# Products of a pair added in PSUM, two of them issued among the next pair's, in a hybrid decoder block

## The chip, the cores and the metric

The kernel runs on one core of a Trainium2 chip. The metric is the device time of one execution in microseconds (us), the median of several runs. Everything is float32 at the boundary; the matrix products are made of float32r parts, as told below.

## What is computed

One decoder layer on 1024 positions of width 1024:

```python
u  = rmsnorm(x)
P  = u @ W_in            # [gate_a | gate_s | B_a | C_a | v_a | z | xBC | dt]
A  = W_a_out( B_a * causal_dwconv3( C_a * v_a ) )
S  = W_s_out( GroupRMSNorm( SSD(conv4(xBC)) * silu(z) ) )
h  = x + W_o( sigmoid(gate_a) * A + sigmoid(gate_s) * S )
v  = rmsnorm(h)
h  = h + W_down( silu(causal_dwconv3(v W_1) + b) * (v W_3) )
out = rmsnorm(h)
```

SSD is the chunked state-space scan: 32 heads in 4 groups, 8 chunks of 128 positions. The inner width of z and of the x part of xBC is 2048, that of the feed-forward part 2816.

## The kernel before

**Tiling.** Channels lie on the 128 partitions, positions along the free axis, so a projection makes one tile of 128 channels by 1024 positions. Two such tiles, a *pair*, are made together. The pair is a 2 by 2 block product (two halves of the contraction, two halves of the positions, two output tiles) done with seven block products instead of eight, in the manner of Strassen and Winograd. The combinations of the activations (a11, a12, a22, s1 to s4; `COMBOS`, L195) are made once for u and once for v. The combinations of the weights (t1 to t4, by L295, L296, L297 and L314 on POOL) are made for each pair.

**A product** (`product`, L253) is twelve matmuls of 128x128 by 128x512. Each operand is split in a high float32r part (a cast on ACT, L148) and the rest (a subtraction on POOL or DVE, L149), and hi x hi, hi x lo and lo x hi are added over four slices of the contraction. The split weights go to one of 13 buffers ("w"), so about six products can be prepared ahead.

**A pair** (`Pair`, L265) loads its first raw weight tile r1 when it is made. `first` runs a11 and a12: a11 is copied out of PSUM by ACT (L285, m1), and DVE adds a12 to it (L287). `operands` loads r2 and makes t1 to t3. `second` runs s1, s2, s3, a22 and s4, and DVE adds the seven results up as it takes them out of PSUM (L308, L311, L312, L313, L316, L318). Each product has a PSUM bank of its own. There are 8 banks: four tagged "mm" (a11, a12, s2, s3) and four tagged "sd" (s1, a22, s4, and all that the SSD chunks need: px, pb, pc, pd, po, pst, pn, pr).

**Which pairs there are.** Three gate pairs at the head (`head`, whose first two products run while u is still being prepared), 8 pairs in `BEFORE`, 29 in `BESIDE`, then, after the output projections, 22 feed-forward pairs (names "up"; `ffn_first`, L969, and the loop at L1010). The kinds in the mixer: xb (xBC, followed by a convolution of four taps on DVE, L539, and silu, and written to memory `ssd_in`), z (silu, also to `ssd_in`), ca (names "cv": C_a and v_a, product and three taps), ba (times ca's result, to `tad`), gs and ga (gates, tanh; tile names "g" and gt). Output tiles live in pools: "s4", 3 buffers (xb, ca's product, ba, also the sums of W_down and the first tile of a feed-forward pair), and "b4", 3 buffers in the mixer (z, gates, convolved tiles). "c2" has 6 half tiles, "t2" 3, raw weights ("raw") 3 buffers of a whole tile.

**SSD beside the pairs.** `BESIDE` is the stretch in which SSD chunks run between products. A clock (`tick`, L328) counts products. Chunk s has its stages at ticks `D0 + DSTEP * s` plus an offset from `STAGES` (L54): loads of the decay matrix m (from `acd`, issued on ACT's queue) and of its inputs (from `ssd_in`) 9 ticks ahead, the relu and exp of m on ACT (L642, L643) 6 ahead, transposes (px, L648) 4 ahead, the matmuls pd, po and pst (L690 to L703) at 0, the sums of squares 3 behind and the norm (pn, L733; a power on POOL, L739; pr, L743) 6 behind. The chunk's number c needs the tiles of its group: for group 0 those are xb 0 to 3, 16 and 20 and z 0 to 3.

**After the mixer.** `y_a` (L816) and `s_out` (L852) are the output projections of A and S, `out_proj` (L882) that of the merge. Beside them runs `w_sums` (L789): it loads two tiles of W_down into two "s4" tiles, combines them on DVE and POOL (L784, L787; tile name wd) and writes them to `td`. After the feed-forward pairs come four sweeps (names d) for W_down.

**What sets the order.** Each engine runs its own queue strictly in order. A planner makes the queues when the program is built: it goes by the order of the program text as a priority and by when operands, buffers and banks would be ready in its own estimate of times. An instruction that comes early in an engine's queue but waits for something late holds all that stands behind it. Loads of weights and stores are issued on SP's queue, the SSD's loads and the stores of convolved tiles and gates on ACT's.

## Time and profile before

| | |
|---|---|
| median of 3 runs | 2004.32 us (2004.31 to 2005.55) |
| the profiled execution | 2004.03 us |
| its span, first to last instruction | 2002.3 us |
| mean granted clock of TensorE | 0.986 |
| head and mixer pairs on PE | to 987 us |
| y_a, s_out, out_proj on PE | 988 to 1347 us |
| feed-forward pairs on PE | 1351 to 1782 us |
| W_down on PE | 1782 to 1994 us |

The page of a profile gives each engine's busy time (PE is TensorE's matmuls, PEld its weight loads, DVE VectorE, ACT ScalarE, POOL GpSimd, SP the engine that only issues here). A row of a window gives, for a stretch of time, the busy time and number of instructions of PE, PEld, DVE, ACT and POOL, the clock granted to TensorE (1.00 is full), the mean busy share of the DMA engines and what they moved. A row of waits reads: engine, tile and line that waited, what ended the wait, the sum of those waits in us, how many, the longest. A row of the timeline gives start, duration, engine, line, operation, tiles (out<-in), shapes, count, and in brackets the idle time of the engine just before it and what ended it. Tile names carry the pair's kind: pt2xb is the product s2 of an xb pair, pb11cv the product a11 of a ca pair, pt4 is a22, pb22 is s4, pt1 is s1.

### The profile page before, as it was taken

The numbers are of one execution on the slowest core, as the hardware profiler recorded it, in microseconds if no ns is written. First come the engines' busy times: TensorE is split into PE (matmuls) and PEld (weight loads), VectorE is DVE, ScalarE is ACT, GpSimd is POOL, SyncE is SP. The second block draws the span as 40 slices with busy tenths as digits, with TensorE's granted clock in tenths as the row PEclk, the third lists the DMA queues.
The fourth block names the chain that finished last, engine by engine and source line by source line (L and its number), as shares of the span: only waits on it lengthen the run. The fifth ranks groups of instructions, "written<-read, shape, count | busy, mean of one in ns | idle before, by whom it ended". The sixth has DMA issues, their size and how long they took to land.

```text
span 2002.3 us, 26005 instructions
## 1 busy us (share of the span) xinstructions
PE 1923.3 (96%) x8986; PEld 1575.2 (79%) x8986; DVE 1450.9 (72%) x1616; ACT 918.0 (46%) x1697; POOL 1292.9 (65%) x931
## 2 busy tenths in 40 slices
PE   6899989999999999998999999988999999999998
PEld 5778877788788778776788888877888888887886
DVE  8956886787888778786884724379877788884445
ACT  5354445556655855444443323354433333343434
POOL 7667776776767677677545423368887888853542
PEclk9999999999999999999999999998999999999999
DMA  4244234444534554387897645442322244477654
GB/s 153 51 141 143 95 121 153 148 152 144 190 119 151 167 168 144 113 267 254 317 409 251 225 151 188 159 165 81 130 85 102 104 153 153 153 242 261 217 184 157
DMA packets 180179, 338.46 MB, mean 169 GB/s; under 512 B 15280, under 2 KB 87760, under 8 KB 179024
## 3 DMA queue, kind: packets, MB, share of 16 engines
q1 hardware_dynamic: 93264, 253.95, 37.1%
q10 hardware_dynamic: 86784, 82.85, 13.0%
q8 instruction: 71, 1.16, 0.2%
q14 instruction: 60, 0.49, 0.1%
HBM read 247.34 MB, written 89.41 MB: 168 GB/s over the span
## 4 chain that ended last, share of the span: by engine, by line
PE 64%; DVE 14%; DMA 7%; issue 5%; POOL 4%; ACT 4%; ACTq 0%; SPq 0%; POOLq 0%; DVEq 0%
PE so L259 9%; PE ya L259 4%; DVE cv L539 4%; PE pt2up L259 3%; PE pt3up L259 3%; PE pb22up L259 3%; PE pt4up L259 3%; PE pb11up L259 3%; PE pt1up L259 3%; PE pb21up L259 3%; PE d L1031 2%; PE d L1032 2%; PE d L1033 2%; DMA wd<-in_w_down 1%; PE wo L904 1%
## 5 line engine op out<-in xcount | busy, mean ns | idle before, releaser
L539 DVE SCALAR_TENSOR_TENSOR cv<-xbc,scw,cv 128x1024 f32<-128x1024 f32 x72 | 128.8, 1800 | 20.8 <-ACT cv L535 20.5
L642 ACT ACTIVATE m<-m,tk 128x128 f32<-128x128 f32 x256 | 79.1, 391 | 101.0 <-DMA m<-acd 88.5
L539 DVE SCALAR_TENSOR_TENSOR fcv<-fci,fcw,fcv 128x1024 f32<-128x1024 f32 x44 | 85.9, 1953 | 28.5 <-ACT fcv L535 28.5
L149 POOL TENSOR_TENSOR l_ws<-raw_ws,h_ws 128x512 fp32r<-128x512 f32 x32 | 46.4, 1450 | 74.6 <-PE so L259 43.1
L148 ACT CAST h_ws<-raw_ws 128x512 fp32r<-128x512 f32 x64 | 39.4, 622 | 99.1 <-PE so L259 67.5
L259 PE MATMUL so<-yh,h_ws 128*128 128x512 f32 x256 | 68.8, 391 | 0.0
L259 PE MATMUL so<-yl,h_ws 128*128 128x512 f32 x256 | 68.6, 389 | 0.0
L259 PE MATMUL so<-yh,l_ws 128*128 128x512 f32 x256 | 68.5, 389 | 0.0
L149 POOL TENSOR_TENSOR l_wo<-raw_wo,h_wo 128x512 fp32r<-128x512 f32 x24 | 31.6, 1316 | 53.9 <-PE wo L905 36.5
L149 DVE TENSOR_TENSOR l_wo<-raw_wo,h_wo 128x512 fp32r<-128x512 f32 x24 | 25.2, 1050 | 51.7 <-ACT h_wo L148 26.9
L661 ACT ACTIVATE xe<-px,tk 128x64 f32<-128x64 f32 x256 | 55.5, 326 | 13.2 <-DVE xd L654 13.2
L148 ACT CAST h_wo<-raw_wo 128x512 fp32r<-128x512 f32 x48 | 29.6, 621 | 65.5 <-PE wo L905 32.7
L149 DVE TENSOR_TENSOR l_ws<-raw_ws,h_ws 128x512 fp32r<-128x512 f32 x32 | 26.0, 816 | 41.6 <-PE so L259 27.7
L259 PEld LDWEIGHTS so<-yl,h_ws 128*128 128x128 f32 x256 | 48.1, 188 | 10.0
L259 PEld LDWEIGHTS so<-yh,l_ws 128*128 128x128 f32 x256 | 48.1, 188 | 10.0
L259 PEld LDWEIGHTS so<-yh,h_ws 128*128 128x128 f32 x256 | 47.8, 188 | 9.7
L672 DVE TENSOR_TENSOR m<-m,cb 128x1024 f32<-128x1024 f32 x32 | 52.6, 1644 | 0.4
L149 POOL TENSOR_TENSOR l_wa<-raw_wa,h_wa 128x512 fp32r<-128x512 f32 x16 | 27.3, 1704 | 37.7 <-ACT h_wa L148 18.5
L903 PE MATMUL wo<-h_wo,mh 128*128 128x512 f32 x128 | 49.9, 391 | 1.2 <-ACT h_wo L148 1.2
L546 ACT ACTIVATE cv<-cv 128x1024 f32<-128x1024 f32 x24 | 25.5, 1062 | 55.1 <-DVE cv L539 55.1
L904 PE MATMUL wo<-l_wo,mh 128*128 128x512 f32 x128 | 50.0, 391 | 0.0
L905 PE MATMUL wo<-h_wo,ml 128*128 128x512 f32 x128 | 49.7, 391 | 0.0
(1063 smaller groups left out, 6710.4 us busy)
## 6 DMA issues: line engine op xcount, KB each, us to landing
m<-acd ACTq DMA_DIRECT2D x32, 512.0 KB, 5.5
raw_ws<-in_w_s_out SPq DMA_DIRECT2D x32, 512.0 KB, 4.2
ssd_in<-cv ACTq DMA_DIRECT2D x24, 512.0 KB, 2.6
in<-ssd_in ACTq DMA_DIRECT2D x32, 384.0 KB, 4.1
raw_wo<-in_w_o SPq DMA_DIRECT2D x24, 512.0 KB, 3.4
wd<-in_w_down SPq DMA_DIRECT2D x22, 512.0 KB, 6.1
td<-wd SPq DMA_DIRECT2D x44, 256.0 KB, 4.3
raw_1up<-in_w_up SPq DMA_DIRECT2D x22, 512.0 KB, 3.2
```

The source lines that it names most:

```text
L148: act.copy(hi, v)
L149: (eng or pool).tensor_tensor(lo, v, f32(hi), op=ALU.subtract)
L259: pe.matmul(ps, wt[:, k, :], ct[:, k, :], start=(start and n == 0), stop=(stop and n == 11),)
L539: dve.scalar_tensor_tensor(cv, ci[:, j : j + SEQ], w[:, j : j + 1], cv, op0=ALU.mult, op1=ALU.add)
L642: act.activation(m[:, h, :], m[:, h, :], AF.Relu, bias=a)
L661: act.activation(xe[:, hc], px[:, hc], AF.Copy, scale=tk[:, 2, cc, q, g * HG + h : g * HG + h + 1],)
L672: dve.tensor_tensor(m, m, cb.unsqueeze(1).to_broadcast([P, HG, P]), op=ALU.mult)
L903: pe.matmul(pss[t], mh, wh, start=k == 0, stop=False)
L904: pe.matmul(pss[t], mh, wl, start=False, stop=False)
L905: pe.matmul(pss[t], ml, wh, start=False, stop=k == NK - 1)
L1031: pe.matmul(ps, aa[0][:, ts], bb[0], start=k == 0, stop=False)
L1032: pe.matmul(ps, aa[0][:, ts], bb[1], start=False, stop=False)
```

## The change

- A pair's products are added in PSUM. a11, s2, s3 and a22 go into one "mm" bank one after the other (t4 has its sign turned, so that a22 is added too); ACT copies the running sum out after a11, s2, s3 and a22 (`so_far`). s1 and s4 share another "mm" bank. a12 has an "sd" bank. What DVE still adds is a12 (to the copy of a11), s1 to the sum after s3, and the bank of s1 and s4 to the sum after s2. The copy of a11 goes into the output tile itself (`hold`). Pairs whose first products run early (three at the head, two feed-forward) don't hold the bank of a11: it is copied to m1 as before, s2 opens a new bank, and DVE adds m1 to each running sum.
- The order of products is a11, a12, the previous pair's a22, s2, the previous pair's s4, s1, s3 (`then`); a pair's last two products, and what is done with its outputs (`done`), come in the next pair. `then(None)` closes the mixer's and the feed-forward part's row of pairs.
- t1, t3 and t4 are made in place, over the raw weights, t4 with the others; "t2" has one buffer, "raw" four. `y_a` takes its gh from "c2".
- `BEFORE` has 6 pairs and `BESIDE` 31, in another order, three of the five gate pairs between the other kinds instead of all at the end; `D0` is 17 instead of 11.

```diff
--- before
+++ after
@@ -31,7 +31,7 @@
 GA, GS, BA, CA, VA, ZZ, XB, BB, CB = 0, 8, 16, 24, 32, 40, 56, 72, 76
 NIN = 80 * P
-NRAW, NW, NBIG, NB4, NC2, NT2, NROW = 3, 13, 14, 3, 6, 3, 6
+NRAW, NW, NBIG, NB4, NC2, NT2, NROW = 4, 13, 14, 3, 6, 1, 6
 LO_DVE = ("t1", "b22")
...
@@ -40,17 +40,17 @@
 BEFORE = (
-    ("xb", 16), ("z", 0), ("xb", 18), ("z", 2), ("xb", 20), ("xb", 22), ("xb", 0), ("xb", 2),
+    ("xb", 16), ("z", 0), ("xb", 20), ("xb", 0), ("z", 2), ("xb", 2),
 )
 BESIDE = (
-    ("xb", 4), ("z", 4), ("xb", 6), ("z", 6), ("ca", 0), ("ca", 1), ("ba", 0),
-    ("xb", 8), ("z", 8), ("xb", 10), ("z", 10), ("ca", 2), ("ca", 3), ("ba", 2),
-    ("xb", 12), ("z", 12), ("xb", 14), ("z", 14), ("ca", 4), ("ca", 5), ("ba", 4),
-    ("ca", 6), ("ca", 7), ("ba", 6), ("gs", 0), ("gs", 2), ("gs", 4), ("gs", 6), ("ga", 6),
+    ("xb", 4), ("z", 4), ("xb", 6), ("z", 6), ("xb", 18), ("gs", 0), ("xb", 22), ("z", 8),
+    ("xb", 8), ("z", 10), ("xb", 10), ("gs", 2), ("ca", 0), ("ca", 1), ("ba", 0), ("z", 12),
+    ("xb", 12), ("z", 14), ("xb", 14), ("gs", 4), ("ca", 2), ("ca", 3), ("ba", 2),
+    ("ca", 4), ("ca", 5), ("ba", 4), ("ca", 6), ("ca", 7), ("ba", 6), ("gs", 6), ("ga", 6),
 )
-D0, DSTEP = 11, 6
+D0, DSTEP = 17, 6
 STAGES = LOAD_M, LOAD_IN, DECAY, TRANS, LOAD_Z, DIAG, SQUARES, NORM = -9, -9, -6, -4, -3, 0, 3, 6
...
@@ -250,7 +250,8 @@
             dve.tensor_tensor(a12[i], a12[i], s1[i], op=ALU.subtract)
             put("s4", i, a12[i])
-    def product(ps, c, w, start=True, stop=True):
+    def product(ps, c, w, start=True, stop=True, held=False):
         hi, lo = (t.rearrange("p (k c) -> p k c", k=4) for t in w)
         n = 0
...
@@ -258,69 +259,108 @@
             for k in range(4):
                 pe.matmul(
                     ps, wt[:, k, :], ct[:, k, :],
-                    start=(start and n == 0), stop=(stop and n == 11),
+                    start=(start and n == 0), stop=(stop and n == 11), skip_group_check=held,
                 )
                 n += 1
     class Pair:
-        def __init__(self, A, src1, src2, name, pool=None):
+        def __init__(self, A, src1, src2, name, d1, d2=None, done=None, pool=None):
             self.A, self.src2, self.name = A, src2, name
+            self.d1, self.d2, self.done = d1, d2, done
             self.r1 = load(src1, f"1{name}", pool)
-        def prod(self, c, v, nm, f=mm_tile):
+            self.started = False
+        def prod(self, c, v, nm, ps=None):
             name = self.name
-            ps = f(f"p{nm}{name}")
+            new = ps is None
+            if new:
+                ps = (sd_tile if nm == "b21" else mm_tile)(f"p{nm}{name}")
             eng = dve if nm in LO_DVE else pool
-            product(ps, self.A[c], wsplit(v, f"{nm}{name}", eng))
+            product(ps, self.A[c], wsplit(v, f"{nm}{name}", eng), new, held=True)
             tick()
             return ps
-        def first(self, d1, late=False):
-            self.d1 = d1
+        def first(self, late=False, hold=True):
+            self.started = True
             p = self.prod("a11", self.r1[:, :HALF], "b11")
-            self.m1 = c2(f"m1{self.name}")
+            self.m1 = self.d1[:, :HALF] if hold else c2(f"m1{self.name}")
             act.copy(self.m1, p)
+            self.hold, self.u = hold, p if hold else None
             p = self.prod("a12", self.r1[:, HALF:], "b21")
-            dve.tensor_tensor(d1[:, :HALF], self.m1, p, op=ALU.add)
+            dve.tensor_tensor(self.d1[:, :HALF], self.m1, p, op=ALU.add)
             if not late:
                 self.operands()
         def operands(self):
-            name, b11 = self.name, self.r1[:, :HALF]
-            self.r2 = load(self.src2, f"2{name}")
-            self.t1, self.t2, self.t3 = (t2(f"t{i}{name}") for i in (1, 2, 3))
-            pool.tensor_tensor(self.t1, self.r2[:, :HALF], b11, op=ALU.subtract)
-            pool.tensor_tensor(self.t2, self.r2[:, HALF:], self.t1, op=ALU.subtract)
-            pool.tensor_tensor(
-                self.t3, self.r2[:, HALF:], self.r2[:, :HALF], op=ALU.subtract
-            )
-        def second(self, d2):
-            name, m1, d1 = self.name, self.m1, self.d1
-            b21, t1, tb = self.r1[:, HALF:], self.t1, self.t2
-            b22 = self.r2[:, HALF:]
-            p5 = self.prod("s1", t1, "t1", sd_tile)
-            p = self.prod("s2", tb, "t2")
-            u2 = c2(f"u2{name}")
-            dve.tensor_tensor(u2, m1, p, op=ALU.add)
-            p = self.prod("s3", self.t3, "t3")
-            u3 = c2(f"u3{name}")
-            dve.tensor_tensor(u3, u2, p, op=ALU.add)
-            dve.tensor_tensor(u2, u2, p5, op=ALU.add)
-            dve.tensor_tensor(d2[:, HALF:], u3, p5, op=ALU.add)
-            pool.tensor_tensor(tb, tb, b21, op=ALU.subtract)
-            p = self.prod("a22", tb, "t4", sd_tile)
-            dve.tensor_tensor(d1[:, HALF:], u3, p, op=ALU.subtract)
-            p = self.prod("s4", b22, "b22", sd_tile)
-            dve.tensor_tensor(d2[:, :HALF], u2, p, op=ALU.add)
-    def pair(A, src1, src2, name, d1, d2):
-        p = Pair(A, src1, src2, name)
-        p.first(d1)
-        p.second(d2)
+            name = self.name
+            r1, r2 = self.r1, load(self.src2, f"2{name}")
+            (b11, b21), (b12, b22) = ([r[:, h] for h in halves] for r in (r1, r2))
+            self.t1, self.t2, self.t3, self.t4, self.b22 = b11, t2(f"t2{name}"), b12, b21, b22
+            pool.tensor_tensor(self.t1, b12, b11, op=ALU.subtract)
+            pool.tensor_tensor(self.t2, b22, self.t1, op=ALU.subtract)
+            pool.tensor_tensor(self.t3, b22, b12, op=ALU.subtract)
+            pool.tensor_tensor(self.t4, b21, self.t2, op=ALU.subtract)
+        def so_far(self, o):
+            if self.hold:
+                act.copy(o, self.u)
+            else:
+                dve.tensor_tensor(o, self.m1, self.u, op=ALU.add)
+        def s2(self):
+            self.u = self.prod("s2", self.t2, "t2", self.u)
+            self.u2 = c2(f"u2{self.name}")
+            self.so_far(self.u2)
+        def s1(self):
+            self.v = self.prod("s1", self.t1, "t1")
+        def s3(self):
+            self.prod("s3", self.t3, "t3", self.u)
+            u3 = c2(f"u3{self.name}")
+            self.so_far(u3)
+            dve.tensor_tensor(self.d2[:, HALF:], u3, self.v, op=ALU.add)
+        def a22(self):
+            self.prod("a22", self.t4, "t4", self.u)
+            self.so_far(self.d1[:, HALF:])
+        def s4(self):
+            self.prod("s4", self.b22, "b22", self.v)
+            dve.tensor_tensor(self.d2[:, :HALF], self.u2, self.v, op=ALU.add)
+            self.done()
+    last = [None]
+    def then(p):
+        q, last[0] = last[0], p
+        if p is None:
+            q.a22()
+            q.s4()
+        elif p.started:
+            p.s2()
+            if q is not None:
+                q.a22()
+            p.s1()
+            if q is not None:
+                q.s4()
+            p.s3()
+        else:
+            p.first()
+            q.a22()
+            p.s2()
+            q.s4()
+            p.s1()
+            p.s3()
     slots, clock = {}, [None]
...
@@ -433,11 +473,11 @@
         for t in (4 + j, 5 + j):
             u_norm(t)
         fill_second(U, [(xs[t], t - 4) for t in (4 + j, 5 + j)], "u", cur["row"])
-        p = Pair(U, w_in[GA + j], w_in[GA + j + 1], f"g{GA + j}", cur["row"])
-        p.first(b4(f"gt{j}"), True)
+        p = Pair(U, w_in[GA + j], w_in[GA + j + 1], f"g{GA + j}", b4(f"gt{j}"), pool=cur["row"])
+        p.first(True, False)
         head.append(p)
-    p = Pair(U, w_in[GA + 4], w_in[GA + 5], f"g{GA + 4}")
-    p.first(s4("gt4")[:, :SEQ], True)
+    p = Pair(U, w_in[GA + 4], w_in[GA + 5], f"g{GA + 4}", s4("gt4")[:, :SEQ])
+    p.first(True, False)
     head.append(p)
     head[0].operands()
...
@@ -552,16 +592,20 @@
         for ci in cis:
             pool.memset(ci[:, 0:3], 0.0)
         d = [ci[:, 3 : 3 + SEQ] for ci in cis]
-        pair(U, w_in[XB + t], w_in[XB + t + 1], f"xb{t}", *d)
-        for i in range(2):
-            conv4(cis[i], t + i)
+        def done():
+            for i in range(2):
+                conv4(cis[i], t + i)
+        then(Pair(U, w_in[XB + t], w_in[XB + t + 1], f"xb{t}", *d, done))
     def z_pair(t):
         zs = [b4(f"z{t + i}") for i in range(2)]
-        pair(U, w_in[ZZ + t], w_in[ZZ + t + 1], f"z{t}", *zs)
-        for i, z in enumerate(zs):
-            act.activation(z, z, AF.Silu)
-            act.dma_start(xd_[(t + i) // 4][:, 6 + (t + i) % 4, :], z)
+        def done():
+            for i, z in enumerate(zs):
+                act.activation(z, z, AF.Silu)
+                act.dma_start(xd_[(t + i) // 4][:, 6 + (t + i) % 4, :], z)
+        then(Pair(U, w_in[ZZ + t], w_in[ZZ + t + 1], f"z{t}", *zs, done))
     taken = {}
...
@@ -601,9 +650,9 @@
     for i, p in enumerate(head):
         if i:
             p.operands()
-        d2 = b4(f"gt{2 * i + 1}")
-        p.second(d2)
-        gates_done((p.d1, d2), gad, 2 * i)
+        p.d2 = b4(f"gt{2 * i + 1}")
+        p.done = lambda p=p, i=i: gates_done((p.d1, p.d2), gad, 2 * i)
+        then(p)
     decays(dt_ps)
     rows_.close()
     ssp = mixer.enter_context(tc.tile_pool(name="ssp", bufs=1))
...
@@ -773,6 +822,7 @@
     clock[0] = 0
     for item in BESIDE:
         run(*item)
+    then(None)
     while slots:
         tick()
     clock[0] = None
...
@@ -821,7 +871,7 @@
             for q in range(2):
                 w = wsplit(raw[:, halves[q]], f"wa{hf}{j}{q}", pool if q else dve)
                 product(ps, ta[q], w, start=q == 0, stop=q == 1)
-            gh = t2(f"ga{hf}{j}")
+            gh = c2(f"ga{hf}{j}")
             sp.dma_start(gh, gad[:, j, sl])
             dve.scalar_tensor_tensor(gh, gh, 1.0, ps, op0=ALU.add, op1=ALU.mult)
...
@@ -1007,18 +1058,22 @@
         sub(s4t, a, s2, pool)
         sp.dma_start(s4d[k], s4t)
-    for i in range(NFF):
-        if i >= 2:
-            ffn_first(i)
-        ci = cis.pop(i)
-        h3 = b4(f"h3_{i}")
-        ffn.pop(i).second(h3)
+    def ffn_done(i):
+        ci, h3 = cis.pop(i), ffn.pop(i).d2
         cv = b4(f"fcv{i}")
         taps(cv, ci, fcw[:, i, :], fcb[:, i : i + 1])
         act.activation(cv, cv, AF.Silu)
         dve.tensor_tensor(cv, cv, h3, op=ALU.mult)
         sp.dma_start(gd[i], cv)
         g_sums(i, cv, h3)
+    for i in range(NFF):
+        if i >= 2:
+            ffn_first(i)
+        ffn[i].d2 = b4(f"h3_{i}")
+        ffn[i].done = lambda i=i: ffn_done(i)
+        then(ffn[i])
+    then(None)
```

ca_pair, ba_pair and gate_pair are changed like z_pair: what followed `pair(...)` is now in a `done()` handed to `Pair`.

More of the change, by code (lines that the diff above doesn't have):

```diff
@@ L573, in ca_pair, with done @@
         pv = pr[:, 2 : 2 + SEQ]
-        pair(U, w_in[CA + i], w_in[VA + i], f"cv{i}", cc, pv)
-        dve.tensor_tensor(pv, pv, cc, op=ALU.mult)
-        dve.tensor_scalar(cc, pv, caw[:, i, 2:3], None, op0=ALU.mult)
-        for j in range(2):
-            dve.scalar_tensor_tensor(
-                cc, pr[:, j : j + SEQ], caw[:, i, j : j + 1], cc, op0=ALU.mult, op1=ALU.add
-            )
-        taken[i] = cc
+        def done():
+            dve.tensor_tensor(pv, pv, cc, op=ALU.mult)
+            dve.tensor_scalar(cc, pv, caw[:, i, 2:3], None, op0=ALU.mult)
+            for j in range(2):
+                dve.scalar_tensor_tensor(
+                    cc, pr[:, j : j + SEQ], caw[:, i, j : j + 1], cc, op0=ALU.mult, op1=ALU.add
+                )
+            taken[i] = cc
+        then(Pair(U, w_in[CA + i], w_in[VA + i], f"cv{i}", cc, pv, done))
     def ba_pair(i0):
         bs = [s4(f"ba{i0 + i}")[:, :SEQ] for i in range(2)]
-        pair(U, w_in[BA + i0], w_in[BA + i0 + 1], f"ba{i0}", *bs)
-        for i in range(2):
-            cc = taken.pop(i0 + i)
-            dve.tensor_tensor(cc, cc, bs[i], op=ALU.mult)
-            sp.dma_start(tad[:, i0 + i, :], cc)
+        def done():
+            for i in range(2):
+                cc = taken.pop(i0 + i)
+                dve.tensor_tensor(cc, cc, bs[i], op=ALU.mult)
+                sp.dma_start(tad[:, i0 + i, :], cc)
+        then(Pair(U, w_in[BA + i0], w_in[BA + i0 + 1], f"ba{i0}", *bs, done))
     def gate_pair(b, dst, j):
         gt = [b4(f"gt{b + j + i}") for i in range(2)]
-        pair(U, w_in[b + j], w_in[b + j + 1], f"g{b + j}", *gt)
-        gates_done(gt, dst, j)
+        then(Pair(
+            U, w_in[b + j], w_in[b + j + 1], f"g{b + j}", *gt, lambda: gates_done(gt, dst, j)
+        ))
     def gates_done(gts, dst, j):
@@ L971, in ffn_first @@
         pool.memset(ci[:, 0:2], 0.0)
-        ffn[i] = Pair(V, w_up[i], w_up[NFF + i], f"up{i}")
-        ffn[i].first(ci[:, 2 : 2 + SEQ], late)
+        ffn[i] = Pair(V, w_up[i], w_up[NFF + i], f"up{i}", ci[:, 2 : 2 + SEQ])
+        if i < 2:
+            ffn[i].first(late, False)
     vs = [(v_norm(t), t - 4) for t in (6, 7)]
```

## The prediction

> **What bounds the kernel now.** I read the page first, then the table of windows, then the waits of PE, then single stretches of the timeline.
>
> ```profile
> span 2002.3 us, 26005 instructions
> PE 1923.3 (96%) x8986; PEld 1575.2 (79%) x8986; DVE 1450.9 (72%) x1616; ACT 918.0 (46%) x1697; POOL 1292.9 (65%) x931
> ```
>
> The profiled execution took 2004.03 us, 1.7 over its span; the median is 2004.32. The change leaves the matmuls as they are (seven products a pair, twelve matmuls each), so it can win only time in which PE stands or runs at a low clock. Where that is, the windows show (columns: busy time of PE, PEld, DVE, ACT, POOL, granted clock, DMA share, GB/s):
>
> ```profile
> 80.00:280.00 200.00, 195.71 (x860) 161.75 (x859) 142.73 (x144) 89.92 (x136) 137.28 (x105) 0.99 0.37 121
> 280.00:860.00 580.00, 560.62 (x2882) 452.73 (x2881) 468.84 (x571) 332.76 (x767) 412.45 (x305) 0.98 0.48 152
> 860.00:1000.00 140.00, 125.97 (x613) 100.27 (x612) 105.37 (x130) 61.53 (x139) 91.40 (x68) 0.96 0.84 279
> 280.00:320.00 40.00, 34.50 (x159) 27.75 (x158) 28.85 (x31) 21.47 (x40) 27.56 (x22) 0.91 0.39 128
> 1000.00:1040.00 40.00, 40.00 (x178) 33.15 (x177) 33.23 (x34) 17.77 (x26) 16.87 (x11) 1.00 1.03 412
> 1400.00:1760.00 360.00, 360.00 (x1590) 298.19 (x1589) 288.44 (x260) 136.07 (x192) 301.82 (x203) 1.00 0.37 128
> ```
>
> The feed-forward pairs (1400 to 1760) keep PE busy throughout: nothing can be gained there, only lost. In the mixer PE stands 4.3, 19.4 and 14.0 us in the first three rows, and the clock costs about 0.01 x 200 + 0.02 x 580 + 0.04 x 140 = 19 us more: 57 in all, the ceiling of any gain. What it stood for:
>
> ```profile
> engine line waited for: us in total, times, longest us
> PE pr L743 <- POOL yr L739: 6.5, 4, 3.3
> PE px L648 <- DMA in<-ssd_in: 5.5, 1, 5.5
> PE po L697 <- DVE gt L316: 4.4, 2, 3.2
> PE tkp L524 <- DVE gt L313: 4.3, 1, 4.3
> PE pb22g L259 <- DVE gt L316: 3.8, 1, 3.8
> PE pn L733 <- DVE ss L730: 3.2, 3, 1.7
> PE pt4xb L259 <- ACT bk L669: 2.0, 2, 1.5
> PE pc L652 <- DVE gt L316: 1.6, 1, 1.6
> PE pt1g L259 <- DVE gt L318: 1.4, 1, 1.4
> ```
>
> No data passes from gt (L313, L316, L318) to po, pc, pb22g or tkp, nor from bk to pt4: these are waits for one of the four "sd" banks, which pairs and SSD chunks share. The worst stretch shows what held DVE:
>
> ```profile
> L784 DVE TENSOR_TENSOR wd<-wd x11: 679/1218/1785, 862.1 to 1069.2; 128x512 f32<-128x512 f32 x11
> DVE wd L784 <- DMA wd<-in_w_down: 18.8, 6, 4.9
> 910.88 1.58 DVE L784 TENSOR_TENSOR wd<-wd 128x512 f32<-128x512 f32 x1 [3.01 <-DMA wd<-in_w_down]
> 915.05 0.67 DVE L316 TENSOR_TENSOR gt<-u3g,pt4g 128x512 f32<-128x512 f32 x1
> 915.78 2.08 PE L259 MATMUL pb22g<-us4h,h_b22g 128*128 128x512 f32 x4 [3.82 <-DVE gt L316]
> ```
>
> The W_down sums (w_sums) begin at 862, when the last ba pair frees its s4 tiles while five gate pairs are still to come. DVE stands in its queue for their loads (18.8 us between 880 and 1000), L316 comes late, the bank comes late, PE stops 3.82 us and then runs at half clock.
>
> **The change, part by part.** The prices of single pieces:
>
> ```profile
> 119.08 2.72 PE pt2xb L259 x12
> L285 ACT COPY m1xb<-pb11xb x12: 562/587/642, 117.0 to 658.7; 128x512 f32<-128x512 f32 x12
> L308 DVE TENSOR_TENSOR u2xb<-m1xb,pt2xb x12: 673/679/689, 121.8 to 673.3; 128x512 f32<-128x512 f32 x12
> raw_1up<-in_w_up SPq DMA_DIRECT2D x22, 512.0 KB, 3.2
> ```
>
> A product is 2.72 us, an eviction 0.59 on ACT or 0.68 on DVE. 37 mixer pairs and 20 feed-forward pairs hold a11, s2, s3 and a22 in one "mm" bank and s1, s4 in another: DVE evictions fall from 7 to 3, ACT copies rise from 1 to 4. That is 57 x 4 x 0.68 = 155 us off DVE and 57 x 3 x 0.59 = 101 us onto ACT.
>
> **Banks.** s1, a22 and s4 leave "sd"; a pair keeps one short tenancy there (b21). A pair's two "mm" banks live about ten and seven products of seven per pair, 2.4 banks of 4 on average. So the "sd" waits lose their cause: po, pb22g, pc and pt1g are 11.2 us, and the clock of their window 0.04 x 140 = 5.6, 16.8 together. Three of the five gate pairs now stand between the other kinds and ba6 is third from the end, so w_sums starts after it, beside y_a, where PE was full at a DMA share of 1.03 (window 1000 to 1040). Ends 0 and 16.8; I take 12, since part may come back there. tkp: 4.3, but the row work of the decays lies there too; ends 0 and 4.3, taken 3. pt4xb 2.0 goes; pn (3.2) waits for DVE sums, and DVE loses 4 x 0.68 = 2.7 us a pair in the mixer: together 5.2.
>
> **Order of pairs and D0.** Before, xb2 ended at tick 0 and chunk 0 transposed at tick 7; now its s4 is the fifth product after the clock starts and the transposes come at 13: 8 products instead of 7, so 2.7 of px's 5.5 us go. The clock of that window (0.91) cost 3.6, half of it taken: 4.5. SSD starts some 8 products earlier in the stream and ends 8 before its end; that moves no PE work.
>
> **Issuing two products late** adds little by itself; the planner does it already:
>
> ```profile
> 358.95 1.07 PE L259 MATMUL pb11cv<-ua11h,l_b11cv 128*128 128x512 f32 x4
> 361.01 1.20 PE L259 MATMUL pt4z<-ua22h,h_t4z 128*128 128x512 f32 x4
> ```
>
> Here z's a22 runs after the next pair's a11.
>
> **Sums in place, four raw buffers, gh in c2.** POOL does the same four sums. A pair's first raw buffer now lives until a22 is split, in the next pair; the load that follows it still has some four products (10.9 us) against 3.2 us to landing. On SP's queue, in order, a store or another load behind it moves with it. POOL's in-place sum waits for a split that precedes it anyway. y_a takes gh from c2 instead of t2 while PE is full. All at 0, from -2 to +4 if the cover fails.
>
> **The wait that is added.** s2 may not write its bank until ACT has copied a11 out, nor s3 before s2's copy, nor a22 before s3's. Two other products lie between: 5.4 us. Behind a late s2 stand, in PE's order, the previous pair's s4, s1, s3 and the chunk's matmuls; behind ACT's copy stand the high parts of later weights and the chunk's relu, exp and loads. In the feed-forward part the cover holds:
>
> ```profile
> 1479.28 1.07 PE L259 MATMUL pb11up<-va11h,l_b11up 128*128 128x512 f32 x4
> 1480.38 0.59 ACT L285 COPY m1up<-pb11up 128x512 f32<-128x512 f32 x1 [2.06 <-PE pb11up L259]
> ```
>
> ACT is there before the product ends, and the copy is out 0.62 us after it. In the mixer it does not always:
>
> ```profile
> 700.09 1.07 PE L259 MATMUL pb11cv<-ua11h,l_b11cv 128*128 128x512 f32 x4
> 710.91 0.70 ACT L642 ACTIVATE m<-m,tk 128x128 f32<-128x128 f32 x2 [5.34 <-DMA m<-acd]
> 711.22 1.09 PE L259 MATMUL pt2cv<-us2h,h_t2cv 128*128 128x512 f32 x4
> 719.36 0.64 ACT L285 COPY m1cv<-pb11cv 128x512 f32<-128x512 f32 x1
> ```
>
> a11 ended at 701.2; ACT stood 5.34 us for the load of m, did the chunk's work, and copied at 719.4 to 720.0. s2 began at 711.22, since it had a bank of its own. In the changed kernel it would have waited 8.8 us. The planner now knows of the need and should put the copy first, but cannot see a late load. Per mixer the ends are 0 and several such blocks; I take one, 8.8. At the two ends without a following pair a22 has nothing between it and s3's copy: 2 x 0.6 = 1.2.
>
> The Trainium skill's Perfetto Trace Analysis, section Matmuls, advises that independent matmul groups should rotate through different PSUM banks, so that evacuation of one overlaps the next; read against this change, which chains four products in one bank, the sum would be that of rival A. The feed-forward rows speak against that reading there, the rows at 700 for it.
>
> **Sum.** 12 + 3 + 5.2 + 4.5 = 24.7 gained, 8.8 + 1.2 = 10 lost: 14.7 off 2004.0 gives 1989.3, taken as **1989 us** (the median stands 0.3 above the profiled execution, which I leave out).
>
> **Rivals.**
> A. ACT's copies become the bound of the mixer: slower.
>
> ```profile
> L642 ACT ACTIVATE m<-m,tk 128x128 f32<-128x128 f32 x256 | 79.1, 391 | 101.0 <-DMA m<-acd 88.5
> ```
>
> ACT stands 88.5 us for m, some 16 blocks of 5.3. If one in four catches a copy that PE needs, 4 x 8.8 = 35 us are lost against 24.7 - 1.2 = 23.5 gained: 2004 + 12 = 2016. It decides from 23.5 / 8.8 = 2.7 blocks on. For it: the rows at 700. Against it: a copy urgent to PE will be planned earlier, and DVE, which ACT often waits for, is lighter.
> B. The tail's loss only moves: w_sums blocks DVE beside y_a, at a DMA share already at 1.03. The 12 are given back: 2001 to 2004.
> C. The ceiling: with "sd" free and DVE lighter, nearly all mixer waits and their clock go, save POOL's pr (6.5) and half the rest of px and tkp: about 57 - 6.5 - 6 = 44, less the 10 lost, 34: 1970.
>
> **How the numbers follow.** Forecast (1978 to 1998) 0.46, A 0.26, B 0.10, C (1955 to 1978) 0.18. A measurement here tells about 0.2%, 4 us, from no change. Faster 0.46 + 0.18 = 0.64, same 0.10, slower 0.26. The range 1963 to 2019 leaves out the lower third of C and the upper part of A.
>
> **What would show it.** DVE's busy time near 1296, ACT's near 1019, PE's matmuls still 8986 and POOL's sums unchanged. No PE wait for gt or bk; w_sums (L784 on wd) after the last ba pair. Wrong, if PE waits for an ACT copy before s2, s3 or a22 more than twice; if the windows of the feed-forward pairs fall under 40 of 40; or if PE stands in y_a, which it did not.

## The result and the profile after

| | before | after |
|---|---|---|
| median | 2004.32 us (4 runs, 1996.69 to 2005.55) | 1978.89 us (4 runs, 1978.07 to 1979.22) |
| the profiled execution | 2004.03 us | 1979.22 us |
| its span | 2002.3 us | 1976.9 us |

After to before is 0.988, with a 95% interval of 0.9856 to 0.9905: 25.4 us faster, where 15 were forecast. The first lines of the page after:

```profile
span 1976.9 us, 25617 instructions
PE 1915.1 (97%) x8986; PEld 1570.6 (79%) x8986; DVE 1229.7 (62%) x1383; ACT 1003.1 (51%) x1876; POOL 1261.1 (64%) x931
```

The matmuls are the same 8986, DVE has 233 instructions fewer and ACT 179 more. So the instructions changed as the edit says, and the time has to be looked for where PE stands or runs slowly. The windows after (columns as before; PE's busy time is the second number):

```profile
0.00:80.00 80.00, 54.64 (x276) 46.57 (x277) 74.19 (x93) 39.45 (x77) 63.76 (x55) 0.87 0.28 102
80.00:280.00 200.00, 199.72 (x900) 164.52 (x900) 107.89 (x112) 107.79 (x180) 138.04 (x104) 1.00 0.39 130
280.00:860.00 580.00, 568.87 (x2958) 460.83 (x2957) 379.40 (x481) 387.57 (x874) 411.67 (x313) 0.99 0.50 156
860.00:1000.00 140.00, 140.00 (x674) 115.03 (x673) 100.73 (x119) 66.34 (x131) 79.84 (x55) 1.00 0.69 251
1320.00:1400.00 80.00, 67.93 (x276) 54.66 (x277) 58.41 (x59) 32.67 (x56) 63.53 (x46) 0.91 0.25 86
1400.00:1760.00 360.00, 359.15 (x1584) 296.74 (x1583) 203.82 (x186) 162.61 (x247) 259.95 (x190) 1.00 0.40 133
```

In the three mixer rows PE stood 4.3, 19.4 and 14.0 us before; it now stands 0.3, 11.1 and 0.0, and the clock is 0.99 or 1.00. But the first and the fifth row are worse than their counterparts of before, which the prediction did not show:

```profile
0.00:80.00 80.00, 58.70 (x307) 50.34 (x308) 72.52 (x94) 40.08 (x78) 59.10 (x52) 0.96 0.29 102
1320.00:1400.00 80.00, 69.66 (x299) 56.14 (x298) 72.94 (x75) 38.32 (x71) 64.63 (x46) 0.94 0.30 106
```

In the first 80 us PE gets 276 matmuls done instead of 307. Windows at fixed times hold shifted work, so I cut the span at three events instead: the first matmul of an xb pair, of s_out and of a feed-forward pair. They are in the view of a tile's instructions, where "A to B" gives the start of the first and of the last one, and the three numbers before it the shortest, median and longest duration in ns. Before:

```profile
L259 PE MATMUL pb11xb<-ua11h,h_b11xb x48: 388/389/796, 104.3 to 642.0; 128*128 128x512 f32 x48
L259 PE MATMUL so<-yh,h_ws x256: 389/389/477, 1033.9 to 1297.5; 128*128 128x512 f32 x128
L259 PE MATMUL pb11up<-va11h,h_b11up x88: 389/389/775, 1351.4 to 1763.7; 128*128 128x512 f32 x88
```

And after:

```profile
L260 PE MATMUL pb11xb<-ua11h,h_b11xb x48: 387/389/474, 106.6 to 650.8; 128*128 128x512 f32 x48
L260 PE MATMUL so<-yh,h_ws x256: 389/389/477, 1001.0 to 1264.6; 128*128 128x512 f32 x128
L260 PE MATMUL pb11up<-va11h,h_b11up x88: 389/389/776, 1320.8 to 1733.5; 128*128 128x512 f32 x88
```

One correction: the last head pair's a22 and s4, two products of 2.72 us, now run behind the first xb product, so 5.4 us of PE work moved from the head into the mixer. With it the stages are:

| us | before | after | difference |
|---|---|---|---|
| head (to the first xb product) | 104.3 | 106.6 + 5.4 = 112.0 | +7.7 |
| mixer (to the first s_out product) | 929.6 | 894.4 - 5.4 = 889.0 | -40.6 |
| to the first feed-forward product | 317.5 | 319.8 | +2.3 |
| from there to the end of the span | 650.9 | 656.1 | +5.2 |
| span | 2002.3 | 1976.9 | -25.4 |

The mixer gave 40 us, and the stretches outside took 15 back. One wait makes this cut blunt. Before, the last tkp matmuls, which belong to the head's row work, wait 4.3 us behind the first matmul of the xb product, so their wait counts as mixer (timeline of PE):

```profile
104.29 0.48 PE L259 MATMUL pb11xb<-ua11h,h_b11xb 128*128 128x512 f32 x1
109.06 0.60 PE L524 MATMUL tkp<-ident,zt 128*128 128x128 f32 x2 [4.29 <-DVE gt L313]
```

After, they are done without a wait before that product begins:

```profile
106.49 0.38 PE L564 MATMUL tkp<-ident,zt 128*128 128x128 f32 x2
106.62 1.17 PE L260 MATMUL pb11xb<-ua11h,h_b11xb 128*128 128x512 f32 x4
```

Counted in the head, this wait makes the head's difference +3.4 and the mixer's -36.3; the sum stays. The waits of PE show the same two sides (columns as before: sum, times, longest):

```profile
PE ps_dt L455 <- DVE us1l L149: 6.6, 1, 6.6
...
PE pb11xb L260 <- ACT u2xb L314: 3.9, 2, 2.0
...
PE pt2g L260 <- DVE u2g L316: 3.4, 1, 3.4
PE pt2up L260 <- ACT vs2h L148: 3.0, 1, 3.0
PE pt2up L260 <- DVE vs2l L149: 2.5, 1, 2.5
...
PE pr L792 <- POOL yr L788: 2.0, 2, 1.6
PE pb11cv L260 <- ACT u2cv L314: 1.9, 1, 1.9
PE pt2up L260 <- DVE u2up L316: 1.9, 1, 1.9
PE pb11cv L260 <- ACT cc L295: 1.3, 1, 1.3
...
PE pn L782 <- ACT bk L718: 1.0, 1, 1.0
...
PE pb11xb L260 <- ACT u3xb L314: 0.6, 1, 0.6
...
PE pt1g L260 <- DVE gt L330: 0.3, 1, 0.3
```

px, tkp, po, pc, pb22g and pt4xb, 21.6 us before, are gone. The new waits in the mixer are those for ACT's copies (L295, L314; a bank keeps the name of its first product, so s3's matmuls stand under pb11xb): 3.9 + 1.9 + 1.3 + 0.6 = 7.7 us in five waits of at most 2.0. Outside the mixer stand the head (ps_dt, pt2g) and the first feed-forward pairs (pt2up).

### The profile page after: what moved, and what is told of

Read it like the earlier page. It is cut to its first block, busy times and chain, and to the rows that moved or that the text cites. A ratio compares the mean times of both kernels' runs of the same rounds, so it can differ in the third digit from the quotient of the medians.

```text
span 1976.9 us, 25617 instructions
## 1 busy us (share of the span) xinstructions
PE 1915.1 (97%) x8986; PEld 1570.6 (79%) x8986; DVE 1229.7 (62%) x1383; ACT 1003.1 (51%) x1876; POOL 1261.1 (64%) x931
## 4 chain that ended last, share of the span: by engine, by line
PE 83%; DVE 6%; ACT 3%; issue 3%; DMA 2%; POOL 2%; ACTq 0%; SPq 0%; POOLq 0%; DVEq 0%
PE pb11up L260 10%; PE so L260 9%; PE pb11xb L260 6%; PE pt1up L260 5%; PE ya L260 4%; PE pb11z L260 4%; PE pb11cv L260 4%; PE d L1086 3%; PE d L1088 3%; PE d L1087 3%; PE pb21up L260 3%; PE pt1xb L260 2%; PE pb11ba L260 2%; PE pb11g L260 2%; PE pt1cv L260 2%
## 5 line engine op out<-in xcount | busy, mean ns | idle before, releaser
L579 DVE SCALAR_TENSOR_TENSOR cv<-xbc,scw,cv 128x1024 f32<-128x1024 f32 x72 | 122.3, 1700 | 52.4 <-ACT cv L575 50.7
L298 DVE TENSOR_TENSOR fci<-fci,pb21up 128x512 f32<-128x512 f32 x20 | 13.8, 688 | 68.7 <-PE pb21up L260 68.7
L1066 DVE TENSOR_TENSOR fcv<-fcv,h 128x1024 f32<-128x1024 f32 x22 | 49.8, 2262 | 10.1 <-ACT fcv L1065 10.1
L777 DVE TENSOR_TENSOR eb<-eb 128x256 f32<-128x256 f32 x32 | 20.4, 637 | 55.5 <-ACT eb L775 55.4
L149 POOL TENSOR_TENSOR l_t3up<-raw_2up,h_t3up 128x512 fp32r<-128x512 f32 x22 | 29.3, 1332 | 40.1 <-PE pb11up L260 38.6
L767 POOL TENSOR_TENSOR sn<-st,cdb 128x512 f32<-128x512 f32 x24 | 32.9, 1372 | 27.4 <-DVE st L762 27.4
```

Source lines behind the costliest of these rows:

```text
L149: (eng or pool).tensor_tensor(lo, v, f32(hi), op=ALU.subtract)
L579: dve.scalar_tensor_tensor(cv, ci[:, j : j + SEQ], w[:, j : j + 1], cv, op0=ALU.mult, op1=ALU.add)
L1066: dve.tensor_tensor(cv, cv, h3, op=ALU.mult)
```

## Experiments

All times are medians; each batch had its own runs of the kernel before (2004.08, 2003.85 and 2004.62 us), and each ratio is against those.

### The order of pairs and D0, without the adding in PSUM

`e1_order` is the kernel before with the three constants of the change:

```diff
-BEFORE, BESIDE, D0 of before
+BEFORE, BESIDE, D0 of the change
```

(The lists themselves are left out here; they stand in the diff of the change.)

> The kernel before with the changed order of pairs and D0 = 17 alone (BEFORE, BESIDE, D0); seven evictions and the banks as before. By stage the changed kernel won about 6 us between 80 and 280 us, 14 between 280 and 860 and 20 in the last 140 us of the mixer. Theory T (two causes: the sd banks in the middle, w_sums meeting late pairs at the tail): the tail alone is won here, 12 to 20 us, so 1984 to 1992 us, and the waits for sd banks between 280 and 860 stay. Rival R (the adding in PSUM did it all, the order none): 2000 to 2006.

Measured: 1978.01 us (1973.55 to 1980.11), ratio 0.987 (0.9851 to 0.9889). Both theories missed: the order alone gives as much as the whole change. Its windows in the mixer:

```profile
280.00:860.00 580.00, 565.92 (x2926) 457.41 (x2925) 466.48 (x578) 353.42 (x798) 419.76 (x311) 0.99 0.50 156
860.00:1000.00 140.00, 138.09 (x677) 113.03 (x676) 110.46 (x132) 57.36 (x114) 86.70 (x60) 1.00 0.70 250
```

The tail is nearly full, although every "sd" bank is used as before, and DVE does 466 us in the first row as it did in the kernel before.

### The adding in PSUM, in the old order

`e2_sums` is the changed kernel with the old `BEFORE` and `BESIDE`; D0 stays 17.

```diff
-BEFORE, BESIDE of the change
+BEFORE, BESIDE of before
```

> The changed kernel with the order of pairs of before (all five gate pairs at the end), D0 kept at 17. T: the middle is won, the tail is not or only in part, since w_sums again starts beside five gate pairs and holds DVE: 1983 to 1995 us, with L784 on wd before the last pairs. Rival R: 1977 to 1981, the same as the changed kernel. A third reading, that either part alone frees the tail (no sd bank is waited for, so a late DVE costs nothing): also 1977 to 1983, but then with DVE standing for wd in the tail while PE does not.

Measured: 1986.72 us (1985.66 to 1991.25), ratio 0.9923 (0.9901 to 0.9945), as expected. Its tail:

```profile
860.00:1000.00 140.00, 131.57 (x653) 105.95 (x652) 93.46 (x124) 71.73 (x148) 87.82 (x65) 0.99 0.93 324
```

With w_sums early again, from 849.2 us, PE stands 8.4 us here, for DVE and for ACT's copies, though s1, a22 and s4 no longer use "sd".

### D0 alone

`e13_d0` is the kernel before with one number changed, so that it and `e2_sums` differ in the rewriting of the pair alone: the adding in PSUM and what goes with it (two products issued late, the sums in place, the buffers). All of this together is called the adding below.

```diff
-D0, DSTEP = 11, 6
+D0, DSTEP = 17, 6
```

> The kernel before with D0 = 17 alone (order, evictions and banks of before). Reference for the adding in PSUM in the old order, which had D0 = 17 too and took 1986.7. If the later start is worth only the wait for chunk 0's input (px, 5.5 us and 3.4 of clock): 1995 to 2001 us, and the adding in PSUM brings 9 to 14 of its 17. If the chunks' later end costs as much as it wins: 2002 to 2008, and the adding brings all of it.

Measured: 1990.35 us (1989.03 to 1993.87), ratio 0.9934 (0.9911 to 0.9957). Both theories missed again: one number brings 14 us. It brings them in the middle and nothing in the tail:

```profile
280.00:860.00 580.00, 569.20 (x2944) 462.32 (x2943) 467.31 (x578) 333.76 (x773) 424.01 (x312) 0.99 0.50 158
860.00:1000.00 140.00, 124.88 (x614) 99.65 (x614) 107.15 (x138) 66.91 (x141) 90.86 (x65) 0.96 0.91 306
```

PE stands 10.8 us in the first row instead of 19.4 and the clock goes from 0.98 to 0.99, which is another 0.01 x 580 = 5.8: 14.4 in all. The waits px (5.5), pr (6.5) and pt4xb (2.0) are no longer among PE's waits; six ticks later PE no longer arrives before the chunk's inputs and row work. In their place PE waits 4.2 us once for pc and 6.6 us for five smaller things.

These kernels, all with D0 = 17, make a square. The stages are cut as above, the 5.4 us corrected where the adding is in:

| difference to before, us | head | mixer | to feed-forward | rest | span |
|---|---|---|---|---|---|
| D0 alone (`e13_d0`) | -0.5 | -14.1 | 0.0 | -0.4 | -15.0 |
| D0 and order (`e1_order`) | -0.8 | -28.0 | +0.6 | +1.9 | -26.3 |
| D0 and adding (`e2_sums`) | +9.0 | -35.1 | +2.3 | +5.9 | -17.9 |
| all three (after) | +7.7 | -40.6 | +2.3 | +5.2 | -25.4 |

So the adding in PSUM gains 21.0 us of the mixer in the old order (35.1 - 14.1) and 12.6 in the new one (40.6 - 28.0), and outside the mixer it loses 18.1 and 13.5. Its net worth is 2.9 us in the one and -0.9 in the other. These are single executions, and the runs of one kernel lie 5.6 us (`e2_sums`) and 6.6 us (`e1_order`) apart, so no net worth of the adding is shown. The wait of tkp lies behind the cut in `e13_d0` (4.6 us) and `e1_order` (4.3) too, and is gone in the two kernels with the adding. Counted in the head, it leaves 16.4 and 8.3 us of gain in the mixer and 13.5 and 9.2 of loss outside.

### What held the tail: banks, or W_down's sums

`e8_mm` moves a22 and s4 of the kernel before to "mm" banks and leaves all else:

```diff
-            p = self.prod("a22", tb, "t4", sd_tile)
+            p = self.prod("a22", tb, "t4")
...
-            p = self.prod("s4", b22, "b22", sd_tile)
+            p = self.prod("s4", b22, "b22")
```

> The kernel before with a22 and s4 in mm banks instead of sd; everything else, evictions and order, as before. If the sd banks as such were what PE waited for, the waits for gt and bk go (po, pb22g, pc, pt1g, tkp, pt4: some 17 us and part of the half clock) and it takes 1984 to 1995 us. If what counts is that DVE is late, the wait only goes over to the mm banks (b11, b21, t2 of the next pairs): 2000 to 2008.

Measured: 2002.77 us (10 runs), ratio 0.9998 (0.9986 to 1.001): no change, as the second expectation had it. The waits for gt are nearly gone and others have come; two of its PE waits:

```profile
PE pst L703 <- DVE yss L735: 6.3, 3, 3.0
PE pn L733 <- DVE ss L730: 4.6, 4, 2.1
```

They were 0.7 and 3.2 us before. PE still waits for a late DVE; only the thing that it waits on is another. The edit has a side effect: six of a pair's seven products now share the four "mm" banks, and 8.1 us of waits for those (freed by L308 and L311) are new. So it shows that moving two products out of "sd" gains nothing, not what more banks in all would bring. `e9_gates_s4` leaves the banks alone and takes away what made DVE late. The gate pairs' outputs go into "s4" tiles, so w_sums, which needs two of the three, can't begin until the gate pairs are done:

```diff
-        gt = [b4(f"gt{b + j + i}") for i in range(2)]
+        gt = [s4(f"gt{b + j + i}")[:, :SEQ] for i in range(2)]
```

> The kernel before, its order kept, but the five gate pairs at the end take their output tiles from s4 instead of b4, so that w_sums cannot have its two s4 tiles until the gates are done. Theory W (the order wins at the tail because w_sums no longer meets late pairs): most of the 14.0 us of standing and 5.6 us of clock between 860 us and the end of the mixer go, 1986 to 1994 us, and L784 on wd first runs after 950. Rival: DVE is late in the tail of itself (chunks and pairs), w_sums or not: 2000 to 2006.

Measured: 1986.18 us (1982.67 to 1986.85), ratio 0.9905 (0.9886 to 0.9923), 17.7 us faster than its runs of before and inside the range of theory W. Its W_down sums and its tail:

```profile
L784 DVE TENSOR_TENSOR wd<-wd x11: 677/687/694, 985.4 to 1177.1; 128x512 f32<-128x512 f32 x11
860.00:1000.00 140.00, 140.00 (x705) 115.06 (x705) 103.87 (x137) 72.80 (x151) 77.68 (x58) 1.00 0.70 243
```

The sums start at 985 instead of 862 us, and the tail is full at full clock. (The edit also takes load off the "b4" tiles; that wasn't tried apart.) `e10_start` is its counterpart: the new beginning, with xb 18 and 22 put in and D0 = 17, but the gate pairs at the end as before.

```diff
-BEFORE, D0 of before
+BEFORE, D0 of the change
-    ("xb", 4), ("z", 4), ("xb", 6), ("z", 6), ("ca", 0), ("ca", 1), ("ba", 0),
+    ("xb", 4), ("z", 4), ("xb", 6), ("z", 6), ("xb", 18), ("ca", 0), ("xb", 22), ("ca", 1), ("ba", 0),
```

> The kernel before with the early part of the new order alone: BEFORE of 6 pairs, D0 = 17, xb18 and xb22 moved into BESIDE, all gate pairs still at the end. Theory W: the middle (280 to 860) is won in part, where chunk 0 finds its inputs there and DVE's convolutions lie wider apart, some 8 to 12 us; the tail is not: 1992 to 1998 us, and w_sums again begins before the gate pairs. Rival (the early start of the chunks is what counts, since they end before the pairs do): 1978 to 1984.

Measured: 1991.49 us (1987.51 to 1992.2), ratio 0.9929 (0.9906 to 0.9952), half a us under the range of theory W. The middle gains, as with D0 alone, and in its tail PE is busy 126.80 of 140 us at a clock of 0.95, with the sums from 854 us. So the two gains are apart: D0 in the middle, the place of the gate pairs in the tail; the new beginning adds nothing to D0 (1990.35 alone). With D0 = 17 in place the rest of the order brings some 12 us (1990.35 to 1978.01). That is 5 or 6 less than the 17.7 of `e9_gates_s4`, which is another edit and has the old D0; the new place of the gate pairs with the old D0 was not tried. Part of it shows in the middle, where PE stands 14.1 us in `e1_order` and 10.8 with D0 alone.

### Do the free "sd" banks matter to the changed kernel?

`e3_vsd` is the changed kernel with the bank of s1 and s4 in "sd" again:

```diff
-                ps = (sd_tile if nm == "b21" else mm_tile)(f"p{nm}{name}")
+                ps = (sd_tile if nm in ("b21", "t1") else mm_tile)(f"p{nm}{name}")
```

> The changed kernel with the bank of s1 and s4 taken from sd instead of mm: it is held for about seven products, so the chunks have three of four sd banks most of the time. If free sd banks are the cause of the gain: 1988 to 2004 us, with PE waits for sd tiles (px, pd, po, pc) back. If the lighter DVE is the cause: 1977 to 1984.

Measured: 1998.65 us (10 runs), ratio 0.9968 (0.9951 to 0.9985), about 20 us slower than the change, inside the first expectation. Two of its PE waits, for "sd" banks that the chunk's copies (L718) hold:

```profile
PE pb21g L260 <- ACT bk L718: 6.6, 1, 6.6
...
PE pt1xb L260 <- ACT bk L718: 3.0, 2, 2.9
```

Between s1 and s4 of a pair five other products are issued, and the bank that they share is taken all that time. The changed kernel needs it outside "sd". Both results stand together: two products fewer in "sd" bring the kernel before nothing (`e8_mm`), and a long tenancy there costs the changed kernel.

### The wait that was added

`e5_own` issues a22 and s4 in their own pair, behind s3 (the pairs that start early keep their order); the additions in PSUM stay:

```diff
+            if q is None:
+                return
...
+            if q is not None:
+                q.a22()
+                q.s4()
             p.first()
-            q.a22()
             p.s2()
-            q.s4()
             p.s1()
             p.s3()
+            p.a22()
+            p.s4()
+            last[0] = None
```

> The changed kernel with each pair's a22 and s4 issued in the pair itself (a11, a12, s2, s1, s3, a22, s4), so that one product or none lies between two that share a bank. If the cover of two products matters: a copy takes 0.59 us and is late by some us in the mixer, so 37 pairs lose 0.5 to 2 us each, 20 feed-forward pairs up to 0.7 each: 1995 to 2060 us, with PE waits for ACT at s3 and a22. If the planner's interleaving gives the same cover anyway: 1977 to 1985.

Measured: 2025.05 us (2023.6 to 2026.1), ratio 1.0104 (1.0082 to 1.0126): 46 us slower than the change, 21 slower than before, inside the first expectation. The middle, and two waits of its PE:

```profile
280.00:860.00 580.00, 547.73 (x2785) 435.16 (x2782) 394.77 (x451) 366.49 (x824) 402.99 (x292) 0.99 0.46 149
```

```profile
PE pb11g L260 <- ACT u2g L314: 5.0, 1, 5.0
...
PE pb11z L260 <- ACT u3z L314: 1.8, 4, 0.8
```

PE stands 32 us in this row instead of 11. From the first xb product to the first s_out product it takes 941.8 us instead of 894.4 for the same 4415 matmuls. PE stands 29.6 us more, of which 10.1 are waits for running sums (17.8 instead of 7.7), and is busy 17.8 us longer with the same work. That the other waits and the slower matmuls follow from the shared bank is likely, but not shown. The feed-forward pairs stay almost full (359.22 of 360): there the planner puts a product of the next pair between s3 and a22 by itself, as it did before. In the mixer, with chunks in between, it doesn't always. In this kernel a shared bank costs no more than it saves only because other products are issued between two that share it. The Trainium skill's Perfetto Trace Analysis, section Matmuls, advises that independent matmul groups rotate through different banks, so that emptying one overlaps the next, and says that an accumulation group stays in one bank. This run agrees with the advice in direction: where products that share a bank follow each other closely, the waits for copies grow from 7.7 to 17.8 us. That all 46 us come from it, the run doesn't show.

`e4_dve` copies the running sums out with DVE instead of ACT, to see whether ACT's queue is what is late:

```diff
-                act.copy(o, self.u)
+                dve.tensor_copy(o, self.u)
```

> The changed kernel with the running sums (after s2, s3 and a22) copied out by DVE instead of ACT. In the changed kernel PE still waits 7.7 us in the mixer for ACT's copies and loses some 3.4 us of clock behind them. If ACT's queue (standing for m) is what makes them late: those waits go and nothing else comes, 1966 to 1974 us. If DVE is the engine that is short: its three copies a pair cost more than ACT's waits, 1984 to 1996.

Measured: 1975.99 us (1972.86 to 1979.75), ratio 0.9864 (0.9834 to 0.9893): between the two expectations, and no further from the change (2.9 us) than its own runs lie apart. Three of its PE waits:

```profile
PE pb11z L260 <- DVE u3z L314: 2.0, 1, 2.0
PE pb11up L260 <- DVE u3up L314: 1.0, 1, 1.0
...
PE pb11xb L260 <- DVE u3xb L314: 0.7, 1, 0.7
```

With 0.5 for one ACT copy that is left (cc), the waits for running sums are 4.2 us (one of them in the feed-forward part) instead of 7.7, and DVE's busy time is back at 1341. Which of the two engines copies is worth a few us at most.

`e6_s1first` puts s1 before s2 in the pairs that start early, to give their evictions one product more:

```diff
-            p.s2()
+            p.s1()
             if q is not None:
                 q.a22()
-            p.s1()
+            p.s2()
```

> The changed kernel, with s1 ahead of s2 for the pairs that are already started (three at the head, two feed-forward); all others as changed. Against the order alone the changed kernel lost 3 us at the head and 3 at the start of the feed-forward part, where PE waits for us1, vs2 and u2. If s2 standing first is the cause (before, s1 was first and its operand is made first): 1971 to 1976 us, and the waits pt2up and pt2g go. If it is the single t2 buffer or the shared banks there: 1977 to 1981.

Measured: 1979.75 us (1975.68 to 1980.71), ratio 0.9872 (0.9853 to 0.9891): no gain. The wait of pt2g for u2g (L316) grew from 3.4 to 6.6 us, and pt1up now waits 3.1 us for its split weights. The waits only moved.

### DVE's load, and the pairs that start early

`e7_load` puts work without use on DVE in each pair, to give back what the change took off it:

```diff
+            for _ in range(4):
+                dve.tensor_tensor(u3, u3, u3, op=ALU.max)
```

> The changed kernel with four more DVE operations a pair (max of a half tile with itself, nothing reads the result), as many as the adding in PSUM took off DVE. If the lighter DVE pays for the added waits for ACT's copies: the mixer loses 5 to 15 us, 1984 to 1994 us. If DVE's load does not matter with the new order: 1977 to 1982.

Measured: 2014.28 us (2010.44 to 2025.49, 6 runs), ratio 1.0055 (1.0032 to 1.0079), 35 us slower than the change and beyond both expectations. But the load came out twice as heavy as meant; the group of its feed-forward part (busy us, mean ns, idle before):

```profile
L332 DVE TENSOR_TENSOR u3up<-u3up 128x512 f32<-128x512 f32 x88 | 116.1, 1319 | 2.8
```

An operation took 1.0 to 1.3 us in the mean, not 0.68, 306 us in all (the last section says what its duration went with). So it says that the mixer is sensitive to DVE's load, and not that 155 us of it are worth 35. The feed-forward pairs bore it with PE at 360.00 of 360.

`e11_own_banks` lets the five pairs that start early keep a bank for each product, with DVE adding up as before:

```diff
             else:
                 dve.tensor_tensor(o, self.m1, self.u, op=ALU.add)
+                self.m1, self.u = o, None
...
-            self.prod("s3", self.t3, "t3", self.u)
+            self.u = self.prod("s3", self.t3, "t3", self.u)
...
-            self.prod("a22", self.t4, "t4", self.u)
+            self.u = self.prod("a22", self.t4, "t4", self.u)
```

> The changed kernel, but the five pairs that are started early (three at the head, two feed-forward) give s2, s3 and a22 a bank each, and DVE adds them up one after the other as before; all other pairs as changed. If PE's waits for u2 there (pt2g 3.4, pt2up 1.9 and what follows at half clock) are the price of sharing a bank while DVE is busy: 1972 to 1976 us. If not, as with s1 put first: 1977 to 1981.

Measured: 1976.08 us (1975.66 to 1976.5), ratio 0.986 (0.9839 to 0.9881), 2.8 us faster than the change. From the first feed-forward product to the end it takes 651.0 us instead of 656.1, as before the change (650.9). The head did not come back: its first xb product is at 108.8 (106.6 after). So the loss from the beginning of the feed-forward part on goes with the shared bank of the pairs that start early, and the head's loss has another cause.

For the head the trace offers one, which wasn't tried. The a12 of its last pair, with the row work for dt (timeline; start, duration, and the idle time in brackets). Before:

```profile
48.48 1.07 PE L259 MATMUL pb21g<-ua12h,h_b21g 128*128 128x512 f32 x4
...
54.83 0.80 PE L415 MATMUL ps_dt<-us1l,wdt10h 128*128 128x256 f32 x2 [3.00 <-DVE us1l L149]
```

After:

```profile
54.68 0.80 PE L455 MATMUL ps_dt<-us1l,wdt10h 128*128 128x256 f32 x2 [6.62 <-DVE us1l L149]
...
56.76 2.04 PE L260 MATMUL pb21g<-ua12h,h_b21g 128*128 128x512 f32 x4 [0.42 <-DVE own_u L244]
```

PE gets us1l at the same time in both. Before, PE had the product to run while it waited; after, the product stands behind ps_dt in PE's queue, and at half clock.

## Why the prediction was right and where it was not

The sign and the range held (1978.9 in 1963 to 2019); the time fell at the fast edge of the likeliest case, 10 us under the 1989 named. By its steps:

- **What bounds the kernel** held: all gains came out of the 57 us in which PE stood or ran slowly in the mixer. Of those, 40.6 went. That is more than rival C left there (44 - 8.8 = 35). The total fell into the forecast's range and not into C's (1955 to 1978) only because 15.2 us came back outside, where the prediction had counted 1.2.
- **The sum** came out near in part by luck. The order and D0, in it with 4.5 us and a part of the 12, give 26 alone. The adding, from which it had most of the rest, gains 12.6 us of the mixer in the new order and loses 13.5 outside, so one term that was too small and others that were too large met.
- **Banks** named the wrong cause. "The sd waits lose their cause" by leaving "sd" was its first reason, and w_sums its second; the 12 us were taken for both together. `e1_order` and `e9_gates_s4` win the tail with every bank where it was, and `e8_mm` takes two products out of "sd" for nothing. The rows at 910 already had it: DVE stood for a load of wd, and the bank was only where PE met it. The price was low for the same reason: 16.8 was cut to 12, since part might return beside y_a. One wait of this step did go with the adding: that of tkp, taken at 3 us of 4.3, is still 4.3 us in `e1_order` and 4.6 in `e13_d0`, and gone in `e2_sums` and after.
- **Rival B**, that return, did not come: PE is busy 140.00 of 140 us to 1000 and stands nowhere in y_a (before, against what the prediction says, it stood 1.6 us there, for tal), though w_sums still waits for its loads there. Its rows after, from the tile's instructions and from DVE's waits:

```profile
L834 DVE TENSOR_TENSOR wd<-wd x11: 677/692/1774, 929.6 to 1148.4; 128x512 f32<-128x512 f32 x11
```

```profile
DVE wd L834 <- DMA wd<-in_w_down: 13.0, 5, 4.8
```

- **Order of pairs and D0** was the step that was mis-sized most: 4.5 us, with px the only wait reckoned. D0 alone brings 14. The prediction counted one product of slack for px; but the same six ticks also spare pr and pt4xb and the half-clock stretches after them, which it had left in place or booked to the banks and DVE.
- **The wait that is added** was 8.8 us, as one block. It came as five short waits, 7.7 us, with two stretches of at least 3.2 us at half clock behind them, some 3 us more (the granted clock is the third number from the end):

```profile
477.20:480.40 3.20, 3.20 (x12) 2.06 (x12) 1.77 (x3) 1.35 (x3) 2.92 (x3) 0.50 1.00 234
723.00:726.20 3.20, 3.20 (x9) 2.52 (x8) 1.39 (x2) 3.20 (x13) 0.00 (x0) 0.50 0.69 216
```

  The size was right and the shape wrong. What the prediction gave as a sign that it is wrong, more than two such waits, is there, but the waits are so short that they cost no more than the block. Of rival A nothing is seen: no stand of ACT for m, 5.3 us each, reached PE whole.

- **"Issuing two products late adds little by itself"** was judged without the shared bank and is wrong with it: without the late issue the changed kernel takes 46 us more (`e5_own`), all in the mixer.
- **What was left out**: the pairs that start early. The prediction followed `hold` in the code and priced only the two ends. In the trace, five pairs lose in the head and at the start of the feed-forward part, together with the 2.3 us between (no run takes those apart) 15 us, or 11 with the wait of tkp counted in the head.
- **The signs named**: matmuls as said, POOL's 931 instructions unchanged, w_sums (L834) after the last ba pair, from 929.6 us. ACT's 1003 is near the 1019 named. DVE's 1229.7 is 66 under the 1296 named: 221 us less for 233 instructions is 0.95 each, more than the 0.68 of an eviction, so others got shorter too: 22 subtractions for the low part of b22 in the feed-forward pairs took 36.8 us before and 16.9 after. Of the waits for gt and bk 0.3 and 1.0 us remain. The feed-forward windows lost 0.85 of 360 us, at the second of the two ends, where a product of W_down (d) waits 0.8 us for DVE; the a22 that was to wait there doesn't.

Open: which of px, pr and the clock after them makes up the 14 us of D0; why the rest of the order brings less than `e9_gates_s4`; the head's loss. The fastest kernels were `e4_dve` and `e11_own_banks` (1976.0 and 1976.1 us), some 28 us under before and 3 under the change, which for `e4_dve` is less than its own runs lie apart; the two together, or either with a head as before, were not tried.

## What to carry to other kernels

When a change has several parts, measure each alone before explaining the whole: here three constants that set an order gave all 26 us, and the rewriting beside them gained in one stage about what it lost in others. A wait names the thing that was lacking last; before giving PE more of that thing, ask why the instruction that frees it came late. Adding several products in one bank saves evictions. Here it came out even with two other products issued between two that share the bank, and cost 46 us with one or none; other distances were not tried.

## What the runs showed of the hardware that was not expected

A DVE operation of 128x512 with both operands in SBUF has no single duration. Those that `e7_load` adds took from 0.68 to 1.8 us (tile's instructions: shortest, median and longest in ns):

```profile
L332 DVE TENSOR_TENSOR u3up<-u3up x88: 677/1662/1820, 1392.2 to 1801.9; 128x512 f32<-128x512 f32 x88
```

The adds that read one operand from PSUM (L298, L330, L340) took 0.67 to 0.69 us in the same run, every one of the 186. Of the 248 added operations 88 took 0.69 us in the mean, and the other 160 took 0.8 to 1.8. All of the 160 began while POOL was inside an instruction, and only 7 of the 88. Of the adds at L340, 52 of 62 began so too and were no longer for it. DVE's sums of W_down (wd) show the same: of 22, 10 before and 13 after took 0.69 us in the mean, the others 1.59, and all of those others began inside an instruction of POOL. No run took POOL's work away, so it is not shown that POOL is the cause. But the evictions that the change removed were DVE's cheap and steady operations, and work of the same shape kept in SBUF cost up to 2.6 times as much.
